# Rotary embedding on one core: one whole batch per transfer, rotated in place, with the tables loaded behind the first batch

## The chip, the cores and the metric

The kernel runs on 1 core of one Trainium2 chip. The metric is the device time in microseconds (us), median of several runs. Before the change it was 322.81 us (322.52 to 323.58, 3 runs). All runs told of here were with a granted clock of 1.0. Each profile is of one run, so the lags read from it below are samples.

Engine names in the profile: DVE is VectorE, POOL is GpSimd. GpSimd computes nothing here; it issues the DMA transfers. A "transfer" below is one issued DMA; a "packet" is one record of a piece of it on one of the core's 16 DMA engines.

## The reference

```python
# x: (8, 2048, 16, 64) float32; cos, sin: (2048, 32) float32
def reference(x, cos, sin):
    x1, x2 = x[..., :32], x[..., 32:]
    cos, sin = cos[None, :, None, :], sin[None, :, None, :]
    return np.concatenate([x1 * cos - x2 * sin, x1 * sin + x2 * cos], axis=-1)
```

67.1 MB are read and 67.1 MB are written, both as float32. On the chip the data are float16: the transfers cast on the way.

## The kernel before

A tile is 1024 positions of one batch: 128 partitions, 8 positions each, so a row of a partition is 8 × 16 × 64 elements, 32 KB of float32 in memory and 16 KB of float16 on the chip. There are 16 tiles, with 16 loads and 16 stores.

```python
J = 8
NT = S // (J * P)                       # 2
io_pool  = ctx.enter_context(tc.tile_pool(name="rope_io", bufs=3))
tmp_pool = ctx.enter_context(tc.tile_pool(name="rope_tmp", bufs=3))
cos_src = cos.rearrange("(t p j) d -> p t (j d)", p=P, j=J)    # 256 rows of 512 B on the chip
...
nc.gpsimd.dma_start(out=cos_sb, in_=cos_src)                    # tables first
nc.gpsimd.dma_start(out=sin_sb, in_=sin_src)
for it in range(NT * B):
    t, b = divmod(it, B)
    s0 = T2 * t
    xt = io_pool.tile([P, J, H, D], f16)
    nc.gpsimd.dma_start(out=xt, in_=x[b, s0:s0+T2].rearrange("(p j) h d -> p (j h d)", j=J))
    ot = io_pool.tile([P, J, H, D], f16)
    v1 = ...; v2 = ...
    nc.vector.tensor_mul(out=ot, in0=xt, in1=cos_b)             # (views cut)
    nc.vector.tensor_mul(out=v1, in0=x2, in1=sin_bb)
    nc.vector.tensor_mul(out=v2, in0=x1, in1=sin_bb)
    nc.vector.tensor_sub(out=o1, in0=o1, in1=v1)
    nc.vector.tensor_add(out=o2, in0=o2, in1=v2)
    nc.gpsimd.dma_start(out=out[b, s0:s0+T2].rearrange(...), in_=ot)
```

Of the kernel before, what the change touches and what calls it, by code (L numbers as in the profile page):

```python
# [1 line left out]

# [4 lines left out]


@with_exitstack  # L10
def kernel(
    ctx: ExitStack,
    tc: tile.TileContext,
    x: bass.AP,
    cos: bass.AP,
    sin: bass.AP,
    out: bass.AP,
):
    nc = tc.nc
    f16 = mybir.dt.float16  # L20

    B, S, H, D = x.shape
    Dh = D // 2
    P = nc.NUM_PARTITIONS
    J = 8
    NT = S // (J * P)
    T2 = J * P

    const_pool = ctx.enter_context(tc.tile_pool(name="rope_const", bufs=1))
    io_pool = ctx.enter_context(tc.tile_pool(name="rope_io", bufs=3))  # L30
    tmp_pool = ctx.enter_context(tc.tile_pool(name="rope_tmp", bufs=3))

    cos_src = cos.rearrange("(t p j) d -> p t (j d)", p=P, j=J)
    sin_src = sin.rearrange("(t p j) d -> p t (j d)", p=P, j=J)
    cos_sb = const_pool.tile([P, NT, J * Dh], f16)
    sin_sb = const_pool.tile([P, NT, J * Dh], f16)
    nc.gpsimd.dma_start(out=cos_sb, in_=cos_src)  # L37
    nc.gpsimd.dma_start(out=sin_sb, in_=sin_src)  # L38

    for it in range(NT * B):  # L40
        t, b = divmod(it, B)
        s0 = T2 * t
        xt = io_pool.tile([P, J, H, D], f16)
        nc.gpsimd.dma_start(  # L44
            out=xt,
            in_=x[b, s0 : s0 + T2].rearrange("(p j) h d -> p (j h d)", j=J),
        )

        ot = io_pool.tile([P, J, H, D], f16)
        v1 = tmp_pool.tile([P, J, H, Dh], f16)  # L50
        v2 = tmp_pool.tile([P, J, H, Dh], f16)

        x1 = xt[:, :, :, 0:Dh]
        x2 = xt[:, :, :, Dh:D]

        cos_b = cos_sb[:, t, :].rearrange("p (j d) -> p j d", d=Dh).unsqueeze(2)
        sin_b = sin_sb[:, t, :].rearrange("p (j d) -> p j d", d=Dh).unsqueeze(2)

        nc.vector.tensor_mul(  # L59
            out=ot.rearrange("p j h (e d) -> p j (h e) d", d=Dh),  # L60
            in0=xt.rearrange("p j h (e d) -> p j (h e) d", d=Dh),
            in1=cos_b.to_broadcast([P, J, 2 * H, Dh]),
        )
        sin_bb = sin_b.to_broadcast([P, J, H, Dh])
        nc.vector.tensor_mul(out=v1, in0=x2, in1=sin_bb)  # L65
        nc.vector.tensor_mul(out=v2, in0=x1, in1=sin_bb)  # L66
        o1 = ot[:, :, :, 0:Dh]
        o2 = ot[:, :, :, Dh:D]
        nc.vector.tensor_sub(out=o1, in0=o1, in1=v1)  # L69
        nc.vector.tensor_add(out=o2, in0=o2, in1=v2)  # L70

        nc.gpsimd.dma_start(  # L72
            out=out[b, s0 : s0 + T2].rearrange("(p j) h d -> p (j h d)", j=J),
            in_=ot,
        )


# [1 line left out]
_INS = ['x', 'cos', 'sin']  # L79
_OUTS = [((8, 2048, 16, 64), 'float32')]  # L80


# [23 lines left out]
```

## Time and profile before

| | before |
|---|---|
| median time | 322.81 us |
| span of the profiled run | 321.2 us |
| VectorE busy | 210.7 us (66%) |
| packets | 5153 |
| HBM bytes over the span | 419 GB/s |

These lines of the page of the kernel before give busy times, then the span in 40 equal slices (each digit a tenth of busy share; GB/s is what the DMA engines moved, where a load counts its float16 side only), then the DMA queue.

```profile
span 321.2 us, 191 instructions
...
DVE 210.7 (66%) x80; POOL 18.9 (6%) x38
...
DVE  0089999970009999994004999999100799999800
...
DMA  6999999999999999999999999999999999999994
GB/s 98 212 218 214 218 275 433 428 445 424 314 226 202 222 220 361 445 433 428 445 231 214 224 204 240 439 416 449 433 373 224 208 216 224 288 449 441 416 449 167
DMA packets 5153, 100.94 MB, mean 314 GB/s; under 512 B 544, under 2 KB 1056, under 8 KB 1056
...
q0 software_dynamic: 5152, 100.93, 100.0%
...
HBM read 67.63 MB, written 67.11 MB: 419 GB/s over the span
...
```

The DMA engines are at 9 tenths in every slice but the first and the last. VectorE has holes, and the view of waits (who waited for whom: us in total, times, longest) shows them as waits for loads.

```profile
...
POOL out_dram L72 <- DVE ot L70: 166.9, 16, 12.8
POOL xt L44 <- DVE v L66: 117.9, 4, 32.1
DVE ot L59 <- DMA xt<-in_x_dram: 93.1, 4, 25.4
...
```

The 93.1 us look like time to win. They are not, because the queue moves data while VectorE waits. The timeline (start, duration, engine, line, operation; idle time before it in brackets) shows the tables issued first, and the first multiplication of each group of four tiles.

```profile
...
1.27 0.82 POOL L37 DMA_DIRECT2D cos_sb<-in_cos_dram  x1 [0.82 <-PEq L101]
2.09 0.73 POOL L38 DMA_DIRECT2D sin_sb<-in_sin_dram  x1
2.81 1.65 POOL L44 DMA_DIRECT2D xt<-in_x_dram  x3
17.63 4.43 DVE L59 TENSOR_TENSOR ot<-xt,cos_sb 128x8192 f16<-128x8192 f16 x1 [17.63 <-DMA xt<-in_x_dram]
...
95.82 4.43 DVE L59 TENSOR_TENSOR ot<-xt,cos_sb 128x8192 f16<-128x8192 f16 x1 [25.36 <-DMA xt<-in_x_dram]
...
173.28 4.42 DVE L59 TENSOR_TENSOR ot<-xt,cos_sb 128x8192 f16<-128x8192 f16 x1 [24.79 <-DMA xt<-in_x_dram]
...
251.26 4.42 DVE L59 TENSOR_TENSOR ot<-xt,cos_sb 128x8192 f16<-128x8192 f16 x1 [25.32 <-DMA xt<-in_x_dram]
...
```

From 95.82 to 173.28 to 251.26 us is 77.5 and 78.0 us for eight transfers of 4.19 MB of float32, 431 GB/s. The Trainium skill ("DMA: Bandwidth & Descriptors", section Where 436 GB/s comes from) gives 435 GB/s as the fabric's ceiling; the trace is within a percent of it. So the kernel is the queue's time plus its two ends.

### The profile page before, as it was taken

The numbers are of one execution on the slowest core, as the hardware profiler recorded it, in microseconds if no ns is written. First come the engines' busy times: TensorE is split into PE (matmuls) and PEld (weight loads), VectorE is DVE, ScalarE is ACT, GpSimd is POOL, SyncE is SP. The second block draws the span as 40 slices with busy tenths as digits, with TensorE's granted clock in tenths as the row PEclk, the third lists the DMA queues.
The fourth block names the chain that finished last, engine by engine and source line by source line (L and its number), as shares of the span: only waits on it lengthen the run. The fifth ranks groups of instructions, "written<-read, shape, count | busy, mean of one in ns | idle before, by whom it ended". The sixth has DMA issues, their size and how long they took to land.

```text
span 321.2 us, 191 instructions
## 1 busy us (share of the span) xinstructions
DVE 210.7 (66%) x80; POOL 18.9 (6%) x38
## 2 busy tenths in 40 slices
DVE  0089999970009999994004999999100799999800
POOL 4001000010000100002000000000200000000000
DMA  6999999999999999999999999999999999999994
GB/s 98 212 218 214 218 275 433 428 445 424 314 226 202 222 220 361 445 433 428 445 231 214 224 204 240 439 416 449 433 373 224 208 216 224 288 449 441 416 449 167
DMA packets 5153, 100.94 MB, mean 314 GB/s; under 512 B 544, under 2 KB 1056, under 8 KB 1056
## 3 DMA queue, kind: packets, MB, share of 16 engines
q0 software_dynamic: 5152, 100.93, 100.0%
q14 instruction: 1, 0.01, 0.0%
HBM read 67.63 MB, written 67.11 MB: 419 GB/s over the span
## 4 chain that ended last, share of the span: by engine, by line
DVE 46%; DMA 27%; issue 20%; POOL 2%; POOLq 0%; DVEq 0%; PEldq 0%
DMA xt<-in_x_dram 27%; DVE ot L59 16%; DVE v L66 8%; DVE v L65 8%; DVE ot L70 8%; DVE ot L69 5%; POOL out_dram L72 1%; POOL cos_sb L37 0%; POOL sin_sb L38 0%; POOLq L101 0%; POOL xt L44 0%; POOLq L72 0%; DVEq L59 0%; PEldq L101 0%; POOLq L44 0%
## 5 line engine op out<-in xcount | busy, mean ns | idle before, releaser
L59 DVE TENSOR_TENSOR ot<-xt,cos_sb 128x8192 f16<-128x8192 f16 x16 | 70.7, 4421 | 93.2 <-DMA xt<-in_x_dram 93.1
L70 DVE TENSOR_TENSOR ot<-ot,v 128x4096 f16<-128x4096 f16 x16 | 36.6, 2285 | 0.0
L65 DVE TENSOR_TENSOR v<-xt,sin_sb 128x4096 f16<-128x4096 f16 x16 | 36.6, 2285 | 0.0
L69 DVE TENSOR_TENSOR ot<-ot,v 128x4096 f16<-128x4096 f16 x16 | 36.6, 2285 | 0.0
L66 DVE TENSOR_TENSOR v<-xt,sin_sb 128x4096 f16<-128x4096 f16 x16 | 36.6, 2285 | 0.0
L72 POOL DMA_DIRECT2D out_dram<-ot x16 | 8.6, 535 | 166.9 <-DVE ot L70 166.9
L44 POOL DMA_DIRECT2D xt<-in_x_dram x16 | 8.6, 550 | 117.9 <-DVE v L66 117.9
L37 POOL DMA_DIRECT2D cos_sb<-in_cos_dram x1 | 0.8, 825 | 0.8 <-PEq L101 0.8
L38 POOL DMA_DIRECT2D sin_sb<-in_sin_dram x1 | 0.7, 733 | 0.0
L90 POOL MEMSET const-float32-0.0<- 128x1 f32 x1 | 0.1, 98 | 0.2 <-issue 0.2
L90 POOL MEMSET const-bfloat16-1.0<- 128x1 bf16 x1 | 0.1, 101 | 0.0
L90 POOL MEMSET const-float32-1.0<- 128x1 f32 x1 | 0.1, 98 | 0.0
L90 POOL MEMSET const-uint8-127<- 128x1 uint8 x1 | 0.1, 98 | 0.0
## 6 DMA issues: line engine op xcount, KB each, us to landing
out_dram<-ot POOLq DMA_DIRECT2D x16, 4096.0 KB, 20.4
xt<-in_x_dram POOLq DMA_DIRECT2D x16, 2048.0 KB, 24.5
cos_sb<-in_cos_dram POOLq DMA_DIRECT2D x1, 128.0 KB, 3.2
sin_sb<-in_sin_dram POOLq DMA_DIRECT2D x1, 128.0 KB, 3.3
```

The source lines that it names most:

```text
L37: nc.gpsimd.dma_start(out=cos_sb, in_=cos_src)
L38: nc.gpsimd.dma_start(out=sin_sb, in_=sin_src)
L44: nc.gpsimd.dma_start(out=xt, in_=x[b, s0 : s0 + T2].rearrange("(p j) h d -> p (j h d)", j=J),)
L59: nc.vector.tensor_mul(out=ot.rearrange("p j h (e d) -> p j (h e) d", d=Dh), in0=xt.rearrange("p j h (e d) -> p j (h e) d", d=Dh), in1=cos ...
L65: nc.vector.tensor_mul(out=v1, in0=x2, in1=sin_bb)
L66: nc.vector.tensor_mul(out=v2, in0=x1, in1=sin_bb)
L69: nc.vector.tensor_sub(out=o1, in0=o1, in1=v1)
L70: nc.vector.tensor_add(out=o2, in0=o2, in1=v2)
L72: nc.gpsimd.dma_start(out=out[b, s0 : s0 + T2].rearrange("(p j) h d -> p (j h d)", j=J), in_=ot,)
L90: nc = _bacc.Bacc("TRN2", target_bir_lowering=False, num_devices=1)
```

## The change

Its intent: transfers of twice the size with 64 KB rows, so half as many of them; no separate output tile, which leaves room for five batch buffers; the tables behind the first load; each store four batches behind its load, so that the queue always holds work. Its core:

```diff
-    J = 8
-    NT = S // (J * P)
+    J = S // P            # 16
+    JC = 8                # VectorE still works on halves of the same size
-    io_pool = ...bufs=3;  tmp_pool = ...bufs=3
+    io_pool = ...bufs=5;  tmp_pool = ...bufs=2
-    nc.gpsimd.dma_start(out=cos_sb, in_=cos_src)
-    nc.gpsimd.dma_start(out=sin_sb, in_=sin_src)
+    def load(b):          # one transfer: x[b], 128 rows of 64 KB
+    def tables():         # sin, then cos, each 128 rows of 1 KB on the chip
+    def rotate(xt):       # per half: v1 = x2*sin; v2 = x1*sin; xw = xw*cos; x1 -= v1; x2 += v2
     ...
+    for b in range(B):
+        tiles[b] = load(b)
+        if b == 0:
+            tables()
+        if b >= 4:
+            nc.gpsimd.dma_start(out=out[b - 4].rearrange(...), in_=tiles[b - 4])
+        rotate(tiles[b])
+    for b in range(B - 4, B):
+        nc.gpsimd.dma_start(out=out[b].rearrange(...), in_=tiles[b])
```

More of the change, by code (lines that the diff above doesn't have):

```diff
@@ L24 @@
     P = nc.NUM_PARTITIONS
-    J = 8
-    NT = S // (J * P)
-    T2 = J * P
+    J = S // P
+    JC = 8
     const_pool = ctx.enter_context(tc.tile_pool(name="rope_const", bufs=1))
-    io_pool = ctx.enter_context(tc.tile_pool(name="rope_io", bufs=3))
-    tmp_pool = ctx.enter_context(tc.tile_pool(name="rope_tmp", bufs=3))
-    cos_src = cos.rearrange("(t p j) d -> p t (j d)", p=P, j=J)
-    sin_src = sin.rearrange("(t p j) d -> p t (j d)", p=P, j=J)
-    cos_sb = const_pool.tile([P, NT, J * Dh], f16)
@@ L36 @@
-    sin_sb = const_pool.tile([P, NT, J * Dh], f16)
-    nc.gpsimd.dma_start(out=cos_sb, in_=cos_src)
-    nc.gpsimd.dma_start(out=sin_sb, in_=sin_src)
-    for it in range(NT * B):
-        t, b = divmod(it, B)
-        s0 = T2 * t
+    io_pool = ctx.enter_context(tc.tile_pool(name="rope_io", bufs=5))
+    tmp_pool = ctx.enter_context(tc.tile_pool(name="rope_tmp", bufs=2))
+    cos_sb = const_pool.tile([P, J, Dh], f16)
+    sin_sb = const_pool.tile([P, J, Dh], f16)
+    def load(b):
         xt = io_pool.tile([P, J, H, D], f16)
@@ L44 @@
         nc.gpsimd.dma_start(
-            out=xt,
-            in_=x[b, s0 : s0 + T2].rearrange("(p j) h d -> p (j h d)", j=J),
-        )
-        ot = io_pool.tile([P, J, H, D], f16)
-        v1 = tmp_pool.tile([P, J, H, Dh], f16)
-        v2 = tmp_pool.tile([P, J, H, Dh], f16)
-        x1 = xt[:, :, :, 0:Dh]
-        x2 = xt[:, :, :, Dh:D]
-        cos_b = cos_sb[:, t, :].rearrange("p (j d) -> p j d", d=Dh).unsqueeze(2)
-        sin_b = sin_sb[:, t, :].rearrange("p (j d) -> p j d", d=Dh).unsqueeze(2)
@@ L59 @@
-        nc.vector.tensor_mul(
-            out=ot.rearrange("p j h (e d) -> p j (h e) d", d=Dh),
-            in0=xt.rearrange("p j h (e d) -> p j (h e) d", d=Dh),
-            in1=cos_b.to_broadcast([P, J, 2 * H, Dh]),
-        )
-        sin_bb = sin_b.to_broadcast([P, J, H, Dh])
-        nc.vector.tensor_mul(out=v1, in0=x2, in1=sin_bb)
-        nc.vector.tensor_mul(out=v2, in0=x1, in1=sin_bb)
-        o1 = ot[:, :, :, 0:Dh]
-        o2 = ot[:, :, :, Dh:D]
-        nc.vector.tensor_sub(out=o1, in0=o1, in1=v1)
@@ L70 @@
-        nc.vector.tensor_add(out=o2, in0=o2, in1=v2)
+            out=xt, in_=x[b].rearrange("(p j) h d -> p (j h d)", j=J)
+        )
+        return xt
+    def tables():
+        nc.gpsimd.dma_start(out=sin_sb, in_=sin.rearrange("(p j) d -> p (j d)", j=J))
+        nc.gpsimd.dma_start(out=cos_sb, in_=cos.rearrange("(p j) d -> p (j d)", j=J))
+    def rotate(xt):
+        for j0 in range(0, J, JC):
+            js = slice(j0, j0 + JC)
+            v1 = tmp_pool.tile([P, JC, H, Dh], f16)
+            v2 = tmp_pool.tile([P, JC, H, Dh], f16)
+            x1 = xt[:, js, :, 0:Dh]
+            x2 = xt[:, js, :, Dh:D]
+            sin_b = sin_sb[:, js, :].unsqueeze(2).to_broadcast([P, JC, H, Dh])
+            cos_b = cos_sb[:, js, :].unsqueeze(2).to_broadcast([P, JC, 2 * H, Dh])
+            nc.vector.tensor_mul(out=v1, in0=x2, in1=sin_b)
+            nc.vector.tensor_mul(out=v2, in0=x1, in1=sin_b)
+            xw = xt[:, js, :, :].rearrange("p j h (e d) -> p j (h e) d", d=Dh)
+            nc.vector.tensor_mul(out=xw, in0=xw, in1=cos_b)
+            nc.vector.tensor_sub(out=x1, in0=x1, in1=v1)
+            nc.vector.tensor_add(out=x2, in0=x2, in1=v2)
@@ L72 @@
+    tiles = {}
+    for b in range(B):
[3 more added lines that the diff above has]
+        if b >= 4:
+            nc.gpsimd.dma_start(
+                out=out[b - 4].rearrange("(p j) h d -> p (j h d)", j=J), in_=tiles[b - 4]
+            )
+        rotate(tiles[b])
+    for b in range(B - 4, B):
         nc.gpsimd.dma_start(
-            out=out[b, s0 : s0 + T2].rearrange("(p j) h d -> p (j h d)", j=J),
-            in_=ot,
+            out=out[b].rearrange("(p j) h d -> p (j h d)", j=J), in_=tiles[b]
```

## The prediction

> **What bounds the kernel now.** The DMA queue. The page's forty slices show DMA at 9 tenths in every slice but the first (6) and last (4); HBM moved 134.7 MB in a 321.2 us span, 419 GB/s. VectorE is busy 210.7 us (66%) and its only long waits are four, 93.1 us in all, for loads of xt (the view of waits). They are not room to gain: while VectorE waits, the slices show 433-445 GB/s of stores, or loads at 202-224 GB/s counted in f16, which is 404-448 of f32 read. One period of four batches lasts 77.5 to 78.0 us (first multiplications at 95.8, 173.3, 251.3 in the timeline) and moves eight transfers of 4.19 MB: 431 GB/s. The Trainium skill ("DMA: Bandwidth & Descriptors", Where 436 GB/s comes from) puts the ceiling at 435 GB/s; the trace agrees within a percent.
>
> **What the change does.**
> - Bytes are the same, f32 on the HBM side of each cast.
> - VectorE work is the same: 80 instructions of the same shapes (4.42 and 2.285 us), 211 us, off the path.
> - Rows double: the trace has one packet per row, 4096 of 32 KB (f32), each recorded at 1.227 us median; the table's 1 KB packets take 0.060 us. The line through both is about 22 ns a packet plus 27.2 GB/s per engine. If a 64 KB row stays one packet, each engine has 128 packets fewer: 2.8 us. Packet records overlap a little, so start-to-start the packets took nearer 1.217 us, which halves it. Estimate 1.5 to 2.8 us saved.
> - Tables: 512 packets become 256, about 0.4 us less; behind the first load they still pass through the same queue.
> - Does the queue run dry? By my estimate, at 19.4 us a transfer, no: five loads fill the queue to about 101 us. The first store is issued near 50 us (two halves of 13.15 us after a load landing near 22 us, plus waiting for the second load), the second near 78. The sixth load waits for store 0, landing near 120 while store 1 is still moving (19 us of slack); the last load is issued near 197 with a store running. It lands near 236, its rotation ends near 262, and the queue still holds stores to 294.
> - The ends stay: about 2.3 us before the first packet, about 4 us after the last.
>
> **On the critical path:** only the queue's own time: 2 to 3 us of about 312. VectorE's waits change place, not the time.
>
> **Prediction: 320.2 us (before 322.81), range 318.3 to 322.8.** Faster by over 2%: 0.03; within 2%: 0.94; slower by over 2%: 0.03.
>
> **What would show each step.** DMA again 9 tenths throughout, with no dip at 100-200 us: queue never dry. Packets near 2,600 rather than 5,153: rows stay whole; near 4,600: rows are cut and the gain is under 1 us. VectorE busy 211 us again, starting near 23 us instead of 17.6. If the queue ran dry, a slice under 9 would appear before the sixth or eighth load, with a wait of GpSimd for a store.
>
> **What would make it wrong.** Rows of 64 KB cut in two (no gain; near 322.4). Rows 64 KB apart meeting the same HBM channels: the same page (Latency and other measured facts) gives a loss only from a 2 MiB pitch; no trace here shows it. A larger lag of one DMA engine, since the last packets are twice as long. The slack estimate wrong where the sixth load waits on a store: that could cost 5 to 20 us.

## More of the kernel before

The experiments ran in three sets on three chips, each set with the kernel before in its own rounds (medians 323.11, 322.97 and 323.11 us); times from different sets are compared with that in mind.

The opening can be seen in windows (window and its length, DVE busy, POOL busy, clock, DMA share, GB/s):

```profile
...
4.00:5.00 1.00, 0.00 (x0) 0.46 (x1) 1.00 1.77 235
5.00:6.00 1.00, 0.00 (x0) 0.00 (x0) 1.00 1.03 116
6.00:7.00 1.00, 0.00 (x0) 0.00 (x0) 1.00 0.81 147
7.00:8.00 1.00, 0.00 (x0) 0.00 (x0) 1.00 0.65 131
2.00:20.00 18.00, 2.37 (x1) 2.46 (x5) 1.00 0.98 186
...
```

From 5 to 8 us the share is 1.03, 0.81 and 0.65, then it is about 1. A share over 1 is no error: the records of packets overlap, which matters later. Nor does a low share in one such window prove lost time: over the whole of 2 to 8 us the share is 0.92, and 0.93 in the changed kernel. The first x data are behind the tables.

## The result, and the profile after

The changed kernel took 318.94 us (318.86 to 319.02, 4 runs), the kernel before in the same rounds 322.66 us. The ratio is 0.988, 95% interval 0.9865 to 0.9896. Ratios here are the mean time of one kernel's runs over that of the other's of the same rounds, so not quite the ratio of the medians quoted. The gain of 3.7 us is clear of noise. The same lines of the page of the changed kernel:

```profile
span 317.2 us, 164 instructions
...
DVE 210.7 (66%) x80; POOL 9.9 (3%) x22
...
DVE  0009999999999999999069999995009994000000
...
DMA  7979999999999999999999999999999999999996
GB/s 132 256 163 266 207 198 202 260 198 198 198 264 264 397 397 529 397 331 231 231 198 199 380 413 397 454 471 264 198 314 413 397 446 479 397 397 512 413 397 264
DMA packets 2593, 100.93 MB, mean 318 GB/s; under 512 B 288, under 2 KB 544, under 8 KB 544
...
q0 software_dynamic: 2592, 100.93, 99.6%
...
HBM read 67.63 MB, written 67.11 MB: 425 GB/s over the span
...
```

Packets fell to 2593, so a 64 KB row stays one packet; VectorE's 210.7 us did not move. The slices of GB/s are more ragged because bytes are booked in lumps of longer packets; the DMA share is 9 nearly throughout. The view of waits:

```profile
...
POOL xt L37 <- DMA out_dram<-xt: 118.1, 3, 56.4
POOL out_dram L68 <- DVE xt L60: 73.8, 2, 48.0
...
DVE v L55 <- DMA xt<-in_x_dram: 29.9, 2, 20.2
DVE v L55 <- DMA sin_sb<-in_sin_dram: 24.3, 1, 24.3
...
```

VectorE now waits for the tables and then only 29.9 us for loads; GpSimd waits instead. These waits changed place and not the time. The timeline, GpSimd's issues and VectorE's start (a count of x4 or x2 merges neighbours):

```profile
...
1.25 0.67 POOL L37 DMA_DIRECT2D xt<-in_x_dram  x1 [0.80 <-PEq L101]
1.91 0.54 POOL L43 DMA_DIRECT2D sin_sb<-in_sin_dram  x1
...
2.96 2.14 POOL L37 DMA_DIRECT2D xt<-in_x_dram  x4
24.26 2.29 DVE L55 TENSOR_TENSOR v<-xt,sin_sb 128x4096 f16<-128x4096 f16 x1 [24.26 <-DMA sin_sb<-in_sin_dram]
...
53.13 0.54 POOL L68 DMA_DIRECT2D out_dram<-xt  x1 [48.03 <-DVE xt L60]
...
79.41 0.54 POOL L68 DMA_DIRECT2D out_dram<-xt  x1 [25.74 <-DVE xt L60]
...
123.00 0.54 POOL L37 DMA_DIRECT2D xt<-in_x_dram  x1 [43.05 <-DMA out_dram<-xt]
...
200.15 0.54 POOL L37 DMA_DIRECT2D xt<-in_x_dram  x1 [56.42 <-DMA out_dram<-xt]
...
265.27 0.53 POOL L73 DMA_DIRECT2D out_dram<-xt  x1 [46.18 <-DVE xt L60]
...
```

The span fell from 321.2 to 317.2 us. The page does not say where those 4.0 us came from, but the trace's semaphore records do. The Trainium skill ("DMA: Bandwidth & Descriptors", section Why a DMA increments its semaphore by 16 and not by 1) says that in a transfer issued by GpSimd each of the 16 engines posts one increment, whatever its shape. The trace agrees: 34 transfers left 544 increments, 18 left 288. So each transfer has 16 arrival times, and with them one can tell the median engine from the last one. Worked out from these records (us from the span's start; the drain is GpSimd's long DRAIN record, which begins beside the issue of its last store and ends after the last arrival):

```
                                                        before    after
last transfer, median engine arrives                    317.20    315.28   -1.92
last transfer, last engine arrives after the median       1.85      0.47   -1.38
from there to the end of the span                         2.15      1.49   -0.66
  of it: GpSimd's drain ends after the last arrival        1.44      0.78
first load, last engine arrives after the median          1.33      0.30
8.39 MB of x in mid-run, median engine                    19.419    19.383  x16 = -0.58
```

The last line is the mean from the first load's arrival to the last transfer's, less the tables' 1.29 us in the changed kernel. Only 0.58 us of the 4.0 is the queue running faster in mid-run. The rest is at the two ends, and in engines that fell behind. A lag, once there, mostly stays: in the kernel before the last engine arrived 1.31 to 1.37 us after the median at every transfer from the first load of x up to 191 us. (The records don't name the engines.) From the load that arrived at 201 us on it was 1.84 to 1.88. That second step isn't the opening's: with the tables moved (next section) the lag rose at the same place, from 0.13 to 0.67 us. The runs don't show its cause.

### The profile page after: what moved, and what is told of

Same layout as the page of the kernel before. It is cut to its first block, busy times and chain, and to the rows that moved or that the text cites. A ratio compares the mean times of both kernels' runs of the same rounds, so it can differ in the third digit from the quotient of the medians.

```text
span 317.2 us, 164 instructions
## 1 busy us (share of the span) xinstructions
DVE 210.7 (66%) x80; POOL 9.9 (3%) x22
## 2 busy tenths in 40 slices
DMA packets 2593, 100.93 MB, mean 318 GB/s; under 512 B 288, under 2 KB 544, under 8 KB 544
## 4 chain that ended last, share of the span: by engine, by line
issue 34%; DMA 19%; DVE 16%; another core or an unknown queue 13%; POOL 1%; POOLq 0%; DVEq 0%; PEldq 0%
DMA xt<-in_x_dram 12%; DMA sin_sb<-in_sin_dram 7%; DVE xt L58 5%; DVE v L55 3%; DVE xt L60 3%; DVE v L56 3%; DVE xt L59 2%; POOL xt L37 1%; POOL out_dram L68 1%; POOLq L101 0%; POOLq L37 0%; POOLq L73 0%; DVEq L55 0%; PEldq L101 0%
## 5 line engine op out<-in xcount | busy, mean ns | idle before, releaser
L55 DVE TENSOR_TENSOR v<-xt,sin_sb 128x4096 f16<-128x4096 f16 x16 | 36.5, 2284 | 54.2 <-DMA xt<-in_x_dram 29.9
L58 DVE TENSOR_TENSOR xt<-xt,cos_sb 128x8192 f16<-128x8192 f16 x16 | 70.7, 4416 | 0.0
L59 DVE TENSOR_TENSOR xt<-xt,v 128x4096 f16<-128x4096 f16 x16 | 36.5, 2283 | 0.1
L60 DVE TENSOR_TENSOR xt<-xt,v 128x4096 f16<-128x4096 f16 x16 | 36.5, 2283 | 0.0
L37 POOL DMA_DIRECT2D xt<-in_x_dram x8 | 4.4, 568 | 118.9 <-DMA out_dram<-xt 118.1
L68 POOL DMA_DIRECT2D out_dram<-xt x4 | 2.1, 539 | 73.8 <-DVE xt L60 73.8
L73 POOL DMA_DIRECT2D out_dram<-xt x4 | 2.1, 532 | 63.0 <-DVE xt L60 63.0
```

What stands on the lines that cost most here:

```text
L37: nc.gpsimd.dma_start(out=xt, in_=x[b].rearrange("(p j) h d -> p (j h d)", j=J))
L55: nc.vector.tensor_mul(out=v1, in0=x2, in1=sin_b)
L58: nc.vector.tensor_mul(out=xw, in0=xw, in1=cos_b)
L59: nc.vector.tensor_sub(out=x1, in0=x1, in1=v1)
L60: nc.vector.tensor_add(out=x2, in0=x2, in1=v2)
L68: nc.gpsimd.dma_start(out=out[b - 4].rearrange("(p j) h d -> p (j h d)", j=J), in_=tiles[b - 4])
```

## The experiments

Two theories were put to the chip. The packet theory, mine in the prediction: fewer packets is where the gain lies. The opening theory: the tables sent first delay the queue and leave some DMA engines behind for the whole run.

### The order alone, in the kernel before

```diff
-    nc.gpsimd.dma_start(out=cos_sb, in_=cos_src)
-    nc.gpsimd.dma_start(out=sin_sb, in_=sin_src)
...
         nc.gpsimd.dma_start(out=xt, in_=...)
+        if it == 0:
+            nc.gpsimd.dma_start(out=cos_sb, in_=cos_src)
+            nc.gpsimd.dma_start(out=sin_sb, in_=sin_src)
```

> The kernel before, with the two table loads moved behind the first load of x; nothing else. Packet theory (the prediction's: half as many packets is where the gain came from): the order gains nothing, within 0.5 us of before. Opening theory (tables sent first delay the queue and leave one DMA engine 2 us behind the median for the rest of the run): 2 to 3.3 us faster than before, and the spread between the first and the last engine's landing of the first load falls from 2.0 us to under 1.

Measured: 320.55 us against 323.11 in the same rounds, ratio 0.9927 (0.9908 to 0.9946). Moving two lines brought 2.4 us by the ratio, some six to seven tenths of the whole gain (by the ratios and by the medians). At the first load the last engine arrived 0.27 us after the median (1.33 before). One window of the opening, 2 to 20 us (DMA share and GB/s are the last two columns), of this run:

```profile
...
2.00:20.00 18.00, 5.45 (x2) 2.44 (x4) 1.00 1.03 204
...
```

Before had 186 GB/s in that window (last line of its windows above), and the changed kernel as many as this run:

```profile
...
2.00:20.00 18.00, 0.00 (x0) 3.10 (x6) 1.00 0.98 204
...
```

### The tables first again, in the changed kernel

```diff
-        tiles[b] = load(b)
         if b == 0:
             tables()
+        tiles[b] = load(b)
```

> The changed kernel with the tables loaded first again. Packet theory: as the changed kernel, 318.9 us, within 0.5. Opening theory: 1.5 to 3 us slower than the changed kernel (320.5 to 322), with an engine lagging about 2 us from the first load on.

Measured: 320.02 us (319.96 to 321.82). The changed kernel itself gave 318.94 and, run once more below, 319.04. So 1.0 to 1.1 us slower by the medians, less than I had expected, with a lag of 1.17 us at the first load. (By the ratios, 0.9923 against 0.988 and 0.9875, it is 1.4 to 1.6 us; they are of means, and one of the six runs took 321.82.) The sign is that of the opening theory; the size depends on the rest of the kernel.

The arrival times show where it comes from. They are compared at the same point of the work, when 8.39 MB of x and both tables have arrived (us; one profile each; the last row is a run told of further down):

```
                                  median engine   last engine after it
before                                25.89             1.32
before, tables moved                  24.57             0.25
changed                               24.54             0.27
changed, tables first                 24.71             1.17
changed, one table ahead              24.33             0.26
```

Moving the tables in the kernel before won 1.32 us for the median engine and 1.07 us of lag, 2.4 us together, which is the gain by the ratio. In the changed kernel tables first cost the median engine 0.17 us and 0.90 us of lag, 1.07 together, which is the loss by the medians.

### The packets alone

The row is cut by a gap of 32 bytes in the on-chip tile; the number of transfers stays 18. Cut in two and in sixteen:

```diff
+    C = 2              # or 16
+    JR = J // C
+    PAD = 16
-        xt = io_pool.tile([P, J, H, D], f16)
+        xt = io_pool.tile([P, C, JR * H * D + PAD], f16)
         nc.gpsimd.dma_start(
-            out=xt, in_=x[b].rearrange("(p j) h d -> p (j h d)", j=J)
+            out=xt[:, :, 0 : JR * H * D],
+            in_=x[b].rearrange("(p c j) h d -> p c (j h d)", c=C, j=JR),
         )                # stores and VectorE's views likewise
```

> The changed kernel with each 64 KB row cut into two packets of 32 KB (a 32 byte gap in the on-chip tile), still 16 transfers. Packet theory at 22 ns a packet: 128 more packets per engine, 2.8 us slower (321.7); at the half that I allowed, 1.5 us (320.4). Opening theory, with the 4.5 ns a packet that the median engine's period shows (19.419 against 19.383 us for 8.39 MB): 0.6 us slower (319.5).

> The same cut to sixteen packets of 4 KB per row: 1920 more packets per engine. Packet theory at 22 ns: 42 us slower (361). At 4.5 ns: 8.6 us slower (327.5). A straight line through this and the cut in two settles the cost of a packet. VectorE views are cut too; if its instructions keep their times it stays off the path.

Measured: 319.41 us in two (319.32 to 319.51), 325.35 us in sixteen (325.21 to 325.42). Against 319.0 that is 0.4 us for 128 packets more on each engine, 3.2 ns each, and 6.35 us for 1920, 3.3 ns each. So 22 ns is wrong by a factor of 6 to 7, and even 4.5 ns was too much. Part of this is not in the queue's stream: GpSimd's first issue took 0.67 us in the changed kernel, 0.83 cut in two and 1.29 cut in sixteen, and the first packet started at 2.61, 2.82 and 3.28 us. From the first load's arrival to the last transfer's the median engine needed 292.03, 292.24 and 297.30 us, which is 1.8 ns for each of 120 packets more (close to the scatter of one profile) and 2.9 ns for each of 1800. The page of the cut in sixteen says why the recorded durations misled me:

```profile
...
DVE 210.7 (65%) x80; POOL 19.6 (6%) x22
...
DMA packets 33313, 100.93 MB, mean 312 GB/s; under 512 B 288, under 2 KB 544, under 8 KB 33312
...
q0 software_dynamic: 33312, 100.93, 116.2%
...
```

The queue's packets are said to take 116.2% of the 16 engines' span. The median record of a load's 4 KB packet is 0.173 us, which lies on my line of 22 ns plus 27.2 GB/s; but packets follow one another faster than that, so their records overlap. Here the duration of a record is not what the queue pays for a packet; the distance from one packet to the next is. The Trainium skill ("DMA: Bandwidth & Descriptors", section Why small descriptors are slow) names a fixed overhead of about 3 cycles per packet. At that page's 850 MHz of the fabric this would be 3.5 ns; the page doesn't say that the same clock applies, so this is an estimate, but the 2.9 to 3.3 ns of the cut in sixteen are close to it. VectorE kept its 210.7 us.

### The number of transfers

```diff
-        nc.gpsimd.dma_start(out=xt, in_=x[b].rearrange("(p j) h d -> p (j h d)", j=J))
+        xr = x[b].rearrange("(p j) h d -> p j h d", j=J)
+        for h0 in (0, JC):
+            nc.gpsimd.dma_start(out=xt[:, h0 : h0 + JC], in_=xr[:, h0 : h0 + JC])
                          # stores likewise
```

> The changed kernel with each batch moved in two transfers of 32 KB rows (32 transfers of x, as before), tables still behind the first load. Packets alone, as the cut in two measured: 319.4. If the number of transfers costs too: the time from the last landing to the end of the span is 1.49 us with 18 transfers and 2.15 us with 34 in the traces so far, so 320.1, near the 320.55 of the kernel before with its tables moved. If transfers cost nothing, the end stays at 1.5 us.

Measured: 320.29 us (320.04 to 320.39), ratio 0.992. The packets of data are those of the cut in two, 319.41 us in other rounds on another chip, so 16 more transfers (with 256 more completion packets) cost about 0.9 us, by the medians and by the ratios alike. The time from the last arrival to the end of the span was 2.14 us. GpSimd's long drain ended 1.43 to 1.44 us after the last arrival in the four profiles with 34 transfers, 0.78 us in eight with 18 (those of the experiments below among them) and 0.82 us in the one with 19. So about 0.66 us of the gain is a shorter end. The kernel cut in sixteen, with 18 transfers, had 0.33 us: the number of transfers isn't the whole rule.

### The tables' rows

```diff
-    cos_src = cos.rearrange("(t p j) d -> p t (j d)", p=P, j=J)
+    cos_src = cos.rearrange("(p s) d -> p (s d)", p=P)      # sin likewise
-            in_=x[b, s0 : s0 + T2].rearrange("(p j) h d -> p (j h d)", j=J),
+            in_=x[b].rearrange("(p s j) h d -> p s (j h d)", s=NT, j=J)[:, t, :],
                          # stores likewise
```

> The kernel before with each partition holding 16 consecutive positions, so that a table is 128 rows of 1 KB instead of 256 of 512 B; tables still first, x still in 32 KB rows. If the tables' packets are the matter: 1 to 1.3 us faster than before. If their place in the order is: at most 0.5 us faster (the 0.4 us of the prediction), and one engine still lands the first load over 1 us behind the median.

Measured: 322.98 us against 322.97 of before, ratio 1.0006 (0.9985 to 1.0026). No gain from half the table packets is seen, though the interval is too wide to exclude the 0.4 us that I gave to these rows. The last engine was 1.93 us behind the median at the first load. In this one profile the median engine did have the tables and 8.39 MB of x 0.41 us sooner than before (25.48 against 25.89), but the last engine had them 0.2 us later.

### The buffers and the lag of the stores

```diff
-    io_pool = ...bufs=5
+    io_pool = ...bufs=4       # or 3
-        if b >= 4:            # store b - 4
+        if b >= 3:            # store b - 3; or 2 and b - 2
```

> The changed kernel with four batch buffers and stores three behind. By the queue model (19.4 us a transfer, 26.3 us a rotation) store 0 is issued at 53 us, store 1 at 79, the first four loads end near 82, each later issue finds at least one transfer queued: never dry, 318.9, within 0.4 of the changed kernel. If the fifth buffer earns anything, 5 us or more slower.

> The same with three buffers, stores two behind. The model: store 1 is issued near 79 us, just before store 0 ends near 82; the last load waits for store 4 and lands near 276, its rotation ends near 302, while store 6 ends near 296: the queue runs dry for 6 to 8 us near the end, 325 to 328 us.

Measured: with four buffers 319.15 us (318.97 to 319.38), as the model has it; the fifth buffer earns at most 0.1 to 0.2 us, by medians of different rounds. With three, 327.97 us (327.85 to 328.19), inside the range given. The windows of that run show the queue dry where the model put it:

```profile
...
290.00:295.00 5.00, 5.00 (x4) 0.00 (x0) 1.00 0.98 419
295.00:300.00 5.00, 4.97 (x2) 0.00 (x0) 1.00 0.01 0
300.00:302.00 2.00, 2.00 (x2) 0.00 (x0) 1.00 0.00 0
302.00:304.00 2.00, 1.37 (x1) 0.33 (x1) 1.00 0.00 0
304.00:306.00 2.00, 0.00 (x0) 0.20 (x1) 1.00 1.22 524
...
```

The DMA share is 0.01 and 0.00 from 295 to 304 us, while VectorE rotates the last batch, and GpSimd waits for it before the last store:

```profile
...
POOL out_dram L73 <- DVE xt L60: 64.0, 2, 50.5
...
```

So the queue model used in the prediction holds on both sides of its edge.

### What at the head of the queue does the harm

Four runs on one chip: the changed kernel itself; one table ahead of the first load and one behind; the first load cut in a small transfer and the rest; the tables behind the second load.

```diff
# one ahead
+        if b == 0:
+            table_one()
         tiles[b] = load(b)
         if b == 0:
-            tables()
+            table_two()
# small first transfer, in load(0); the other loads stay whole
+            nc.gpsimd.dma_start(out=xt[:, 0:1], in_=xr[:, 0:1])
+            nc.gpsimd.dma_start(out=xt[:, 1:J], in_=xr[:, 1:J])
# tables behind the second load (tiles[1] is not loaded again later)
         if b == 0:
+            tiles[1] = load(1)
             tables()
```

> The changed kernel itself, to have it in the same rounds as the runs beside it: 318.9, within 0.2; ratio to before 0.988.

> The changed kernel with one table ahead of the first load and one behind. If what is ahead of the first load costs in proportion: half of the 1.1 us that both tables ahead cost, 319.5, with an engine 0.6 to 0.8 us behind the median at the first load's landing. If a single small transfer ahead is enough to spoil the opening: 320.0 and over 1 us behind.

> The changed kernel with its first load cut into a first transfer of one position per partition (128 packets of 4 KB) and one of the other fifteen; tables behind. If small packets at the head of the queue are what sets an engine back: 319.5 to 320.2 and an engine over 0.6 us behind the median. If it takes the tables themselves: 319.0, at most 0.1 us over the changed kernel, and at most 0.4 us behind.

> The changed kernel with its tables behind the second load. VectorE starts near 44 us instead of 24, but by the queue model store 0 is then issued near 73 and store 1 near 99, before the five loads end near 103: never dry, 318.9 within 0.3. If VectorE's start matters at all: up to 20 us slower.

Measured: 319.04, 319.08, 318.92 and 319.00 us; ratios 0.9875, 0.9874, 0.9871 and 0.9872, with intervals that cover one another. Both of my guesses for one table ahead were wrong: no cost is seen, nor with a small first transfer. Of what was tried, only both tables ahead of the first load cost anything. At the first load the last engine arrived 0.57, 0.26, 0.31 (the small transfer) and 0.72 us after the median, so a lag of up to 0.7 us there did not show in the time. The window from 2 to 20 us does not settle it. It has 211 GB/s with one table ahead (first line) and 209 with both ahead (second line), against 204 in the changed kernel; the arrival times above tell them apart.

```profile
...
2.00:20.00 18.00, 0.00 (x0) 3.10 (x6) 1.00 1.03 211
...
2.00:20.00 18.00, 0.00 (x0) 3.09 (x6) 1.00 1.05 209
...
```

With the tables behind the second load VectorE starts 20 us later (store 0 issued at 72.76 instead of 53.13 us) and the time is the same: another confirmation that VectorE is off the path.

In every run the first packets of x are stretched: in the changed kernel up to 3.4 us where 2.43 is the median, before up to 2.7 where 1.23 is. Why two short transfers ahead let this stretching fall on the engines unevenly, and one does not, these runs do not show. It stays open.

### All together

| kernel | transfers | packets | median us | lag at first load | lag at the end |
|---|---|---|---|---|---|
| before | 34 | 5153 | 322.66 to 323.11 | 1.33 | 1.85 |
| before, long table rows | 34 | 4897 | 322.98 | 1.93 | 2.39 |
| before, tables moved | 34 | 5153 | 320.55 | 0.27 | 0.64 |
| changed, two transfers per batch | 34 | 4897 | 320.29 | 0.23 | 0.41 |
| changed, rows cut in two | 18 | 4641 | 319.41 | 0.30 | 0.44 |
| changed | 18 | 2593 | 318.94 and 319.04 | 0.30 and 0.57 | 0.47 and 0.72 |
| changed, tables first | 18 | 2593 | 320.02 | 1.17 | 1.19 |

The lags are those of the profiled run, in us; the other runs stand in their sections.

Read from before down the third to the sixth row, the gain falls into steps: about 2.4 us for the order of the tables (by the ratio; 2.6 by the medians), 0.3 for the other differences, 0.9 for fewer transfers and 0.4 for fewer packets (medians of different rounds). That is 4.0 in all; the changed kernel's own ratios give 3.9 and 4.0. The order's share is 1.0 to 1.1 when taken away from the changed kernel instead, so the steps do not add up independently of their order. No version tried is faster than the changed kernel beyond noise.

## Why the prediction was right or wrong

- **The DMA queue bounds the kernel; VectorE's waits are not to be had.** Right. The waits for loads fell from 93.1 to 29.9 us (and 24.3 for the tables, queued behind a load) and the time moved by 1.2%; a start of VectorE 20 us later changed nothing.
- **The queue never runs dry.** Right. The model said stores at 50 and 78 us, the sixth load near 120, the last load landing near 236 and rotated by 262. The timeline shows 53.13, 79.41, 123.00; VectorE took up the last batch when it had landed at 238.46, and the last store was issued at 265.27. The runs with three and four buffers show its edge.
- **64 KB rows stay whole, with no harm from their pitch.** Right: 2593 packets, mid-run 19.383 against 19.419 us per 8.39 MB. The page that the prediction names for the pitch measured the sync and scalar queues, and no pitch under 512 KiB; for 64 KB this run is the evidence.
- **Time.** 320.2 predicted, range 318.3 to 322.8; 318.94 measured, inside it. "Within 2%" was right. The gain was 3.7 us where 2.6 was forecast.
- **Mis-sized: "22 ns a packet", "1.5 to 2.8 us saved".** Measured about 3 ns a packet (2.9 to 3.3 in the cut in sixteen) and about 0.4 us. I fitted durations of records that overlap, saw the overlap, and allowed for only half of it.
- **Mis-sized: tables, "about 0.4 us less".** With the longer rows alone no gain is seen (ratio 1.0006, interval 0.9985 to 1.0026). What I left out beside them was worth more: their place in the order, where I gave no gain at all, brought 2.4 us in the kernel before and 1.0 to 1.1 in the changed one.
- **Wrong: "The ends stay".** The first packet began at 2.79 us before and at 2.61 after (I had taken 2.3 for both). The end got 0.66 us shorter with 18 transfers instead of 34, and the lag of the last engine, which I named only as a risk, fell by 1.38 us.

So the range held with a sum whose largest term was too large and which lacked three others: the tables' place, the number of transfers and the last engine's lag. The two errors were of opposite sign. That the time fell inside the range is partly luck; what was understood is the full queue and its slack.

## What to carry to other kernels

When a queue is full in every slice of the page, look at the gaps before its first bulk transfer and after its last one, and at the last of the 16 engines rather than their mean: where the tables went first, the last engine's lag of the opening (1.17 to 1.93 us) was still there at the end (1.19 to 2.39). Put bulk work at the head of the queue and test small tables behind it. Cost a packet by its distance to the next packet, or by a run with many more packets, not by the length of its record.

## What the Trainium skill lacked or had wrong

- "DMA: Bandwidth & Descriptors", section Measured: about 10.5 ns a packet is given for a transfer of 64 packets, as the floor of one small transfer. It gives no cost of a packet in a full queue; here that was 2.9 to 3.3 ns (rows cut into 4 KB packets).
- The same page, section Where 436 GB/s comes from, says that for transfers between HBM and SBUF the HBM side (about 358 GB/s) binds. Here, with one core running, 8.39 MB took 19.383 us, 433 GB/s, loads and stores alike. The page's own measured table, which it says is of single cores, has 425 GB/s for 16 MB and agrees with the runs.
- I found no page on how a kernel's end depends on the number of its transfers: GpSimd's long drain ended 1.43 to 1.44 us after the last arrival with 34 transfers and 0.78 with 18; 0.33 with 18 transfers and 33313 packets.
- I found no page on what small loads ahead of the first bulk load cost: two table loads of 0.26 MB cost 1.0 to 2.4 us and left the last engine 1.2 to 1.9 us behind the median; with one such load ahead no cost was seen.
- I found no page that says what overlapping packet records do to the reading of a profile: the queue's share reached 116.2% in the profile of the cut in sixteen, and a line through the durations of single records overstated the cost of a packet by a factor of 6 to 7.
